# Query and key projections of the dilated attention by seven block products, with the results kept in DRAM

## The chip, the cores and the metric

The kernel runs on one core of a Trainium2 chip. The metric is the device time of one execution in microseconds (us). The engines are TensorE (PE, matmuls; PEld is its weight load), VectorE (DVE), ScalarE (ACT), GpSimd (POOL) and SyncE (SP, which here only issues DMAs). Each runs its own instructions in order.

## The reference

The kernel computes one encoder layer on 512 tokens of width 1024, in float32:

```python
x = x + 0.5 * swiglu(rmsnorm(x, g1), w1, w3, w2)      # FFN a, inner width 2816
h = rmsnorm(x, mix_norm)
pa, pq, pk, pv, pg = split(h @ w_in)                  # one input projection
# A: pa is (3 of q,k,v) x (3 groups) x (8 heads) x 64; dilations 1, 4, 16; band +-64 steps;
#    groups combined per position by a softmax over their log-sum-exps
# B: grouped-query attention, 8 query heads and 2 key heads of 128, rotary
mix = (sigmoid(pg_A) * (o_A @ P_A) + sigmoid(pg_B) * (o_B @ P_B)) @ w_out
x = x + mix
x = x + 0.5 * swiglu(rmsnorm(x, g2), ...)             # FFN b
out = rmsnorm(x, final_norm)
```

## The kernel before

**Matmuls.** Every float32 matmul is done as three in the fast format fp32r: each operand is split into a high part H and a remainder L, and `mm3` (L206 to L208) adds H·H, H·L and L·H in PSUM. Weights come in tiles of 128x1024 (512 KB): a DMA on SP's queue loads `wr`, ACT casts it to `wh` (L191), DVE computes the remainder `wl` (L192). The rings of these tiles have three buffers each, so loads, casts and remainders run ahead of PE. `order` is the list of weight tiles in the order of use.

**What sets the order.** PE's instructions are issued as the program is written; the other engines' are placed by a scheduler. Two mechanisms mix work on PE. `weave(main, fill)` takes a generator `main` of attention steps, and after each step as many units of `fill` as the step asks for. `fill` is `stream`: it goes through the list `items` of projections, one unit being three 512-column matmuls of a projection. `until(fill, item)` runs fill densely until an item is done. The gaps are GAP_S = 2 units after each pair of score tiles, GAP_V = 4 after each stage of values, GAP_B = 1 after each step of attention B, GAP_X = 8 ahead of the last values of A.

**The projections of the mixer.** `items` before: the values V of the three groups (96 units), then query and key for the four head pairs (6 chunks each, 8 units a chunk), gates 0 to 5, B's projection group 0, gates 6 and 7, B's groups 1 and 2, gates 8 to 15. A chunk of query or key is a bank of 128 features x 512 tokens; its eviction multiplies by R, the reciprocal root mean square of each token (which lies in a permuted order `Rp` for the groups with a dilation), into a tile `qk` in SBUF (L589, L591; nine buffers). Gates go to DRAM (`gate_d`) and are read back later.

**Attention A.** For each head pair `scores_a` computes S from the `qk` tiles (L648), adds the bias W and takes maxima (L653), takes exponentials on ACT (L662), exchanges maxima and sums through DRAM on SP's queue (L672 to L676; the exchange changes the layout between the groups), and computes a factor F (L678 to L688). `values_a` scales P by F (L706), transposes it on PE (T, L717) and multiplies by V (L699). The loop in `mixer` is: `until` the pair's query and key are done, scores of pair hp, values of pair hp - 1. **Attention B** is pipelined over 38 steps: scores, a transpose Tb (L829), its split PTH/PTL (L124, L125), and the matmul with v.

**Seven products.** `strassen`, `right` and `slots` are already in use for w1 and w3 in both FFNs: two feature blocks of 128 and two halves of the tokens (256 columns) and of the inner dimension (512) are the 2x2x2 blocks. The seven steps (A11, S1, S2, A12, S3, S4, A22) each take 24 matmuls of 256 columns. Some steps need sums of weight blocks: POOL's queue adds a block to a loaded one with an accumulating DMA (`wt`, L173), and DVE forms others (`ws`, L190). They also need sums of blocks of h, made once per projection (TH and TL). `slots` interleaves neighbouring pairs of columns.

## Time and profile before

| what | value |
|---|---|
| runs | 1311.12, 1311.21, 1313.84 us; median 1311.21 |
| the profiled execution | 1309.11 us, its span 1307.3 us |
| busy: PE, DVE, ACT, POOL | 1282.6, 838.1, 557.0, 111.9 us |
| granted PE clock, mean | 0.997 |
| DMA | 163.49 MB, mean 125 GB/s |

The span is the time from the first to the last instruction of the profiled execution. Busy times are sums over instructions of an engine; the forty slices and the windows show where in the span they lie. A row of instructions reads: line, engine, operation, output <- inputs, shape, count, busy time, mean of one in ns, and behind the second bar the idle time ahead of them with what ended it. A row of a timeline begins with the start and the duration.

### The profile page before, as it was taken

The numbers are of one execution on the slowest core, as the hardware profiler recorded it, in microseconds if no ns is written. First come the engines' busy times: TensorE is split into PE (matmuls) and PEld (weight loads), VectorE is DVE, ScalarE is ACT, GpSimd is POOL, SyncE is SP. The second block draws the span as 40 slices with busy tenths as digits, with TensorE's granted clock in tenths as the row PEclk, the third lists the DMA queues.
The fourth block names the chain that finished last, engine by engine and source line by source line (L and its number), as shares of the span: only waits on it lengthen the run. The fifth ranks groups of instructions, "written<-read, shape, count | busy, mean of one in ns | idle before, by whom it ended". The sixth has DMA issues, their size and how long they took to land.

```text
span 1307.3 us, 18961 instructions
## 1 busy us (share of the span) xinstructions
PE 1282.6 (98%) x7634; PEld 1112.7 (85%) x7634; DVE 838.1 (64%) x1248; ACT 557.0 (43%) x841; POOL 111.9 (9%) x100
## 2 busy tenths in 40 slices
PE   7999999999999999999999999999999999999997
PEld 5897999899789877777887778888889889988986
DVE  7884688468632346554574899655676847774775
ACT  7551355145422244244233456543475415442553
POOL 3111110010200000000022400000301000100001
PEclk9999999999999999999999999999999999999999
DMA  7865666252323223222322221245637536753321
GB/s 234 239 189 170 176 193 178 97 130 68 110 81 97 97 83 96 82 72 77 113 96 95 82 80 49 96 158 164 194 100 193 175 96 168 176 157 98 96 81 65
DMA packets 75863, 163.49 MB, mean 125 GB/s; under 512 B 11760, under 2 KB 18304, under 8 KB 75776
## 3 DMA queue, kind: packets, MB, share of 16 engines
q1 hardware_dynamic: 63984, 138.12, 32.2%
q0 software_dynamic: 11072, 23.61, 10.1%
q8 instruction: 60, 0.98, 0.3%
q10 hardware_dynamic: 720, 0.55, 0.1%
q14 instruction: 27, 0.22, 0.1%
HBM read 155.87 MB, written 10.04 MB: 127 GB/s over the span
## 4 chain that ended last, share of the span: by engine, by line
PE 85%; DVE 6%; ACT 3%; issue 3%; DMA 2%; POOL 1%; SPq 0%; POOLq 0%; DVEq 0%; ACTq 0%
PE mm L206 23%; PE mm L207 23%; PE mm L208 23%; PE Y L208 2%; PE Y L207 2%; PE Y L206 2%; ACT P L662 2%; DVE wl L192 1%; PE S L648 1%; PE X L206 1%; PE X L208 1%; PE Tb L829 1%; PE X L207 1%; PE mm L699 1%; DVE gg L405 0%
## 5 line engine op out<-in xcount | busy, mean ns | idle before, releaser
L191 ACT CAST wh<-wr 128x1024 fp32r<-128x1024 f32 x157 | 164.3, 1048 | 353.5 <-PE mm L207 243.1
L206 PE MATMUL mm<-hH,wh 128*128 128x512 f32 (+1 forms) x720 | 253.3, 352 | 4.9 <-ACT wh L953 4.9
L208 PE MATMUL mm<-hH,wl 128*128 128x512 f32 (+1 forms) x720 | 249.0, 346 | 1.4 <-DVE wl L954 0.9
L207 PE MATMUL mm<-hL,wh 128*128 128x512 f32 (+1 forms) x720 | 248.4, 345 | 1.0 <-DVE hL L328 0.9
L192 DVE TENSOR_TENSOR wl<-wr,wh 128x1024 fp32r<-128x1024 f32 x157 | 192.3, 1225 | 86.7 <-ACT wh L191 86.6
L206 PEld LDWEIGHTS mm<-hH,wh 128*128 128x128 f32 x720 | 135.7, 188 | 25.4 <-ACT wh L953 4.9
L208 PEld LDWEIGHTS mm<-hH,wl 128*128 128x128 f32 x720 | 135.5, 188 | 19.8 <-DVE wl L954 1.2
L207 PEld LDWEIGHTS mm<-hL,wh 128*128 128x128 f32 x720 | 135.6, 188 | 19.1 <-DVE hL L328 3.2
L207 PE MATMUL mm<-gg,wh 128*128 128x512 f32 (+1 forms) x376 | 143.0, 380 | 2.3 <-DVE gg L405 2.3
L206 PE MATMUL mm<-gg,wh 128*128 128x512 f32 (+1 forms) x376 | 143.4, 381 | 0.2 <-ACT gg L404 0.2
L208 PE MATMUL mm<-gg,wl 128*128 128x512 f32 (+1 forms) x376 | 142.6, 379 | 0.0
L459 DVE TENSOR_TENSOR u<-mm,R 128x512 f32<-128x512 f32 (+1 forms) x52 | 33.8, 649 | 97.2 <-PE mm L208 97.1
L206 PE MATMUL mm<-TH,wh 128*128 128x256 f32 x304 | 85.6, 281 | 2.0 <-DVE c L431 2.0
L207 PEld LDWEIGHTS mm<-gg,wh 128*128 128x128 f32 x376 | 71.0, 189 | 17.4 <-DVE gg L405 3.8
L208 PE MATMUL mm<-TH,wl 128*128 128x256 f32 x304 | 85.5, 281 | 0.0
L207 PE MATMUL mm<-TL,wh 128*128 128x256 f32 x304 | 85.4, 281 | 0.0
L206 PEld LDWEIGHTS mm<-gg,wh 128*128 128x128 f32 x376 | 70.9, 189 | 16.2 <-ACT gg L404 1.0
L208 PEld LDWEIGHTS mm<-gg,wl 128*128 128x128 f32 x376 | 70.8, 188 | 14.0
L206 PE MATMUL mm<-wh,hH 128*128 128x512 f32 x192 | 77.0, 401 | 0.0
L208 PE MATMUL mm<-wh,hL 128*128 128x512 f32 x192 | 76.2, 397 | 0.0
L207 PE MATMUL mm<-wl,hH 128*128 128x512 f32 x192 | 76.2, 397 | 0.0
L191 ACT CAST wh<-wa 128x1024 fp32r<-128x1024 f32 x38 | 39.9, 1050 | 84.4 <-PE mm L207 49.7
(198 smaller groups left out, 2652.0 us busy)
## 6 DMA issues: line engine op xcount, KB each, us to landing
wr<-in_waq SPq DMA_DIRECT2D x24, 512.0 KB, 3.5
wr<-in_w2a SPq DMA_DIRECT2D x22, 512.0 KB, 3.5
wr<-in_w2b SPq DMA_DIRECT2D x22, 512.0 KB, 3.5
wt<-in_w13b SPq DMA_DIRECT2D x20, 512.0 KB, 4.3
wa<-in_w13b SPq DMA_DIRECT2D x20, 512.0 KB, 4.3
wt<-in_w13b POOLq DMA_DIRECT2D x20, 512.0 KB, 5.9
wt<-in_w13a SPq DMA_DIRECT2D x18, 512.0 KB, 3.6
wt<-in_w13a POOLq DMA_DIRECT2D x18, 512.0 KB, 6.0
```

Source lines behind the costliest of these rows:

```text
L191: self.nc.scalar.copy(H, raw)
L192: self.nc.vector.tensor_sub(L, raw, f32(H))
L206: mm(out, lH, rH, start=start, stop=False, skip_group_check=more)
L207: mm(out, lH, rL, start=False, stop=False, skip_group_check=more)
L208: mm(out, lL, rH, start=False, stop=stop, skip_group_check=more)
L459: nc.vector.tensor_mul(u, ps, R)
L648: nc.tensor.matmul(*args, start=True, stop=True)
L662: nc.scalar.activation(sl, sl, AF.Exp, bias=SO[:, 0, li, h:h + 1], scale=1.0, accum_out=SO[:, 0, li, 2 + h:3 + h])
L699: nc.tensor.matmul(oc, v, p, start=st, stop=sp)
L829: nc.tensor.transpose(pt[:, 128 * j:128 * j + 128], P[h, j][:, 128 * k:128 * k + 128], self.ident)
```

## The change

The mixer now begins with `project_qk`. It runs the three value projections of `stream`, and between their units twelve small steps (`tq_steps`) in which ACT and DVE form TQ, four sums of blocks of x times the norm's gain (H and L parts). Then 20 of the 24 query and key chunks are computed by `strassen`: ten (head pair, group) pairs of PAIRS, whose query and key chunk form the two feature blocks, in the order of PAIRS. `evict` collects the products (ACT copies, DVE additions), scales by R (permuted in `acc`, which takes the place of `Rp`) into tiles `qo` of one buffer, and stores each to DRAM (`qk_d`) on POOL's queue. `fetch(hp)` reads a head pair's tiles back into `qk`, on POOL's queue too. The last four chunks (head pair 3, groups 1 and 2) stay in `items` as they were. Now `items` behind the values is: gates 0 to 2, the remaining query and key chunks, gates 3 to 8, B's groups 0, 1 and 2, gates 9 to 15. `until` ahead of the scores is left only for head pair 3, GAP_X goes from 8 to 4, and V gets a pool of its own that is freed ahead of attention B.

```diff
@@ -19,8 +19,10 @@
 BUFS = {"wr": 3, "wa": 3, "ws": 2, "wt": 3, "wh": 3, "whx": 1}
 EARLY = 4
 GROUPS = {"a": (4, 8, 16, 22), "b": (2, 8, 16, 22)}
+PAIRS = ((0, 0), (1, 0), (0, 1), (0, 2), (1, 1), (1, 2), (2, 0), (3, 0), (2, 1), (2, 2), (3, 1), (3, 2))
+NSQ = 10
 STEPS = ("A11", "S1", "S2", "A12", "S3", "S4", "A22")
-GAP_X = 8
+GAP_X = 4
 GAP_V = 4
 GAP_S = 2
 GAP_B = 1
@@ -81,16 +83,21 @@
         self.acc = c.tile([128, T], F32, name="acc")
         self.open_h()
         self.gate_d = self.dram.tile([16, 128, T], F32, name="gate_d")
-        self.items = ([("v", g) for g in range(3)] + [("qk", h) for h in range(4)] + [("g", j) for j in range(6)]
-                      + [("b", 0), ("g", 6), ("g", 7), ("b", 1), ("b", 2)] + [("g", j) for j in range(8, 16)])
-        span = {"v": ("wav", 4), "qk": ("waq", 6), "g": ("wg", 1), "b": ("wb", 4)}
+        self.qk_d = self.dram.tile([2 * NSQ, 128, T], F32, name="qk_d")
+        self.items = ([("v", g) for g in range(3)] + [("sw", 0)] + [("g", j) for j in range(3)]
+                      + [("qk", f) for f in range(NSQ, 12)] + [("g", j) for j in range(3, 9)]
+                      + [("b", g) for g in range(3)] + [("g", j) for j in range(9, 16)])
+        span = {"v": ("wav", 4), "qk": ("waq", 2), "g": ("wg", 1), "b": ("wb", 4)}
         self.order = self.ffn_order("a")
         for kind, n in self.items:
+            if kind == "sw":
+                self.order += [("swq", at) for at in self.slots(range(0, NSQ, 2))]
+                continue
             name, m = span[kind]
             self.order += [(name, m * n + i) for i in range(m)]
         self.order += [("wab", i) for i in range(12)] + [("wo", i) for i in range(8)]
         self.order += self.ffn_order("b")
-        self.raws, self.tiles, self.used, self.wx = {}, [], 0, None
+        self.raws, self.tiles, self.used, self.wx, self.TQ = {}, [], 0, None, None
         self.rings = {k: [] for k in BUFS}
         self.index = {it[:2]: n for n, it in enumerate(self.order)}
         self.kind = [self.home(it) for it in self.order]
@@ -267,8 +274,11 @@
     def right(self, step, k):
         lo, hi = slice(0, 256), slice(256, 512)
         d, cs = {"A11": (k, lo), "A12": (4 + k, lo), "S3": (k, hi), "S4": (4 + k, hi)}.get(step, (0, 0))
-        if cs:
+        if cs and not (self.TQ and step == "S3"):
             return self.hH[d][:, cs], self.hL[d][:, cs]
+        if self.TQ:
+            c = {"S1": 0, "S3": 1, "A22": 2, "S2": 3}[step]
+            return tuple(t[:, k, c, :] for t in self.TQ)
         c = {"S1": 0, "A22": 1, "S2": 2}[step]
         return self.TH[:, c, k, :], self.TL[:, c, k, :]
 
@@ -363,10 +373,10 @@
...
-        nc.vector.tensor_copy(self.Rp.rearrange("p (r m) -> p r m", r=4), self.R.rearrange("p (m r) -> p r m", r=4))
+        nc.vector.tensor_copy(self.acc.rearrange("p (r m) -> p r m", r=4), self.R.rearrange("p (m r) -> p r m", r=4))
         pr = self.aux("rps")
         for r in range(4):
-            nc.tensor.transpose(pr[:, r:r + 1], self.Rp[0:1, 128 * r:128 * r + 128], self.ident[0:1, 0:1])
+            nc.tensor.transpose(pr[:, r:r + 1], self.acc[0:1, 128 * r:128 * r + 128], self.ident[0:1, 0:1])
         nc.vector.tensor_copy(self.r[:, 4:8], pr[:, 0:4])
...
@@ -580,21 +590,16 @@
 
                 yield from self.token("wav", 4 * n, toks, done)
             elif kind == "qk":
-                qk = {}
-                for j, (part, g) in enumerate([(0, 0), (1, 0), (0, 1), (1, 1), (0, 2), (1, 2)]):
-
-                    def done(ps, part=part, g=g):
-                        t = self.ap.tile([128, T], F32, tag="qk", name="qk", bufs=9)
-                        if g == 0:
-                            nc.vector.tensor_mul(t, ps, self.R)
-                        else:
-                            nc.vector.tensor_mul(t.rearrange("p (r m) -> p r m", r=4),
-                                                 ps.rearrange("p (m r) -> p r m", r=4),
-                                                 self.Rp.rearrange("p (r m) -> p r m", r=4))
-                        qk[part, g] = t
-
-                    yield from self.feat("waq", 6 * n + j, done)
-                self.qk[n] = qk
+                hp, g = PAIRS[n]
+                for part in range(2):
+
+                    def done(ps, hp=hp, part=part, g=g):
+                        t = self.qk[hp][part, g] = self.ap.tile([128, T], F32, tag="qk", name="qk", bufs=9)
+                        nc.vector.tensor_mul(t.rearrange("p (r m) -> p r m", r=4),
+                                             ps.rearrange("p (m r) -> p r m", r=4),
+                                             self.acc.rearrange("p (r m) -> p r m", r=4))
+
+                    yield from self.feat("waq", 2 * n + part, done)
             elif kind == "g":
 
                 def done(ps, j=n):
@@ -607,6 +612,107 @@
                 toks = [(lambda t, i=i: t[:, 128 * i:128 * i + 128]) for i in range(4)]
                 yield from self.token("wb", 4 * n, toks, lambda i, b, grp=n: self.rope(grp, i, b))
             self.past.add((kind, n))
+
+    def fetch(self, hp):
+        for f, (h, g) in enumerate(PAIRS[:NSQ]):
+            if h == hp:
+                for part in range(2):
+                    t = self.qk[hp][part, g] = self.ap.tile([128, T], F32, tag="qk", name="qk", bufs=9)
+                    self.nc.gpsimd.dma_start(t, self.qk_d[2 * f + part])
+
+    def tq_steps(self, cp):
+        nc = self.nc
+        raw = {}
+
+        def put(k):
+            raw[k] = cp.tile([128, 4, 256], F32, tag="c1", name="Traw")
+            for e in range(2):
+                d = k + 4 * e
+                nc.scalar.activation(raw[k][:, 2 * e:2 * e + 2], self.x[d].rearrange("p (a n) -> p a n", a=2), AF.Copy,
+                                     scale=self.par[:, G_MIX + d:G_MIX + d + 1])
+
+        def sums(k):
+            b = [raw[k][:, c] for c in range(4)]
+            neg = lambda o, x, y: nc.vector.scalar_tensor_tensor(o, x, -1.0, y, op0=ALU.mult, op1=ALU.subtract)
+            nc.vector.tensor_sub(b[0], b[0], b[1])
+            nc.vector.tensor_sub(b[1], b[3], b[1])
+            neg(b[3], b[3], b[0])
+            neg(b[2], b[3], b[2])
+
+        def part(k):
+            H, L = (t[:, k] for t in self.TQ)
+            nc.scalar.copy(H, raw[k])
+            nc.vector.tensor_sub(L, raw[k], f32(H))
+
+        return [lambda fn=fn, k=k: fn(k) for k in range(4) for fn in (put, sums, part)]
+
+    def project_qk(self):
+        nc, tc = self.nc, self.tc
+        with ExitStack() as ctx:
+            pool = lambda n, **k: ctx.enter_context(tc.tile_pool(name=n, reuse_waits="tile", **k))
+            tp = pool("qT", bufs=1)
+            self.TQ = [tp.tile([128, 4, 4, 256], F32R, name=f"TQ{c}") for c in "HL"]
+            self.wx = pool("wxq", bufs=1)
+            cp, qp = pool("cq", bufs=2), pool("qo", bufs=1)
+            steps = self.tq_steps(cp)
+            hooks = {7: self.stat_r, 12: self.stat_R, 17: self.stat_p}
+            for n, _ in enumerate(self.stream(self.items[:3])):
+                if n in hooks:
+                    hooks[n]()
+                if n > 20 and n % 4 == 0 and steps:
+                    steps.pop(0)()
+            assert not steps
+            c = {}
+
+            def scaled(dst, src, a, perm, neg):
+                src, dst = src.rearrange("p (j n) -> p j n", j=2), dst.rearrange("p (j n) -> p j n", j=2)
+                R = (self.acc if perm else self.R).unsqueeze(1).to_broadcast([128, 2, T])
+                if perm:
+                    src = src.rearrange("p j (m r) -> p j r m", r=4)
+                    dst, R = (t.rearrange("p j (r m) -> p j r m", r=4)[:, :, :, 64 * a:64 * a + 64] for t in (dst, R))
+                else:
+                    dst, R = (t[:, :, 256 * a:256 * a + 256] for t in (dst, R))
+                if neg:
+                    for j in range(2) if perm else (slice(0, 2),):
+                        nc.vector.scalar_tensor_tensor(dst[:, j], src[:, j], -1.0, R[:, j], op0=ALU.mult, op1=ALU.mult)
+                else:
+                    nc.vector.tensor_mul(dst, src, R)
+
+            def store(f, part, t):
+                i = 2 * f + part
+                nc.gpsimd.dma_start(self.qk_d[i:i + 3:2].rearrange("c p n -> p c n"), t.rearrange("p (c n) -> p c n", c=2))
+
+            def evict(f, step, ps):
+                perm = PAIRS[f][1] > 0
+                if step == "A11":
+                    c[f] = (cp.tile([128, 1024], F32, tag="c1", name="c1"), self.tmp.tile([128, T], F32, tag="t", name="c2"))
+                c1, c2 = c[f][:2]
+                lo, hi = c1[:, :T], c1[:, T:]
+                if step == "A11":
+                    nc.scalar.copy(lo, ps)
+                elif step == "S1":
+                    nc.scalar.copy(c2, ps)
+                elif step == "S2":
+                    nc.scalar.copy(hi, ps)
+                elif step == "A12":
+                    nc.vector.tensor_add(lo, ps, lo)
+                elif step == "S3":
+                    nc.vector.tensor_add(c2, ps, c2)
+                elif step == "S4":
+                    nc.vector.tensor_add(hi, ps, hi)
+                    o = qp.tile([128, 1024], F32, tag="qo", name="qo")
+                    scaled(o, lo, 0, perm, False)
+                    scaled(o, hi, 1, perm, False)
+                    store(f, 0, o)
+                else:
+                    o = qp.tile([128, 1024], F32, tag="qo", name="qo")
+                    scaled(o, ps, 0, perm, True)
+                    scaled(o, c2, 1, perm, True)
+                    store(f, 1, o)
+
+            for _ in self.strassen("q", range(0, NSQ, 2), evict):
+                pass
+            self.wx = self.TQ = None
 
     def until(self, fill, item):
         while item not in self.past:
@@ -853,31 +959,33 @@
 
     def mixer(self):
         nc, tc = self.nc, self.tc
-        self.past, self.qk = set(), {}
-        fill = self.stream()
+        self.past, self.qk = set(), {h: {} for h in range(4)}
+        vctx = ExitStack()
+        vp = vctx.enter_context(tc.tile_pool(name="V", bufs=1, side="right", reuse_waits="tile"))
+        self.V = [vp.tile([128, 4, 512], F32, name=f"V{g}") for g in range(3)]
+        self.project_qk()
+        fill = self.stream(self.items[4:])
         with tc.tile_pool(name="oA", bufs=1, reuse_waits="tile") as oa:
             self.oH = [oa.tile([128, T], F32R, name=f"oH{h}") for h in range(4)]
             self.oL = [oa.tile([128, T], F32R, name=f"oL{h}") for h in range(4)]
             with tc.tile_pool(name="A", bufs=1, reuse_waits="tile") as ap:
                 self.ap = ap
-                self.Rp = ap.tile([128, T], F32, name="Rp")
-                self.V = [ap.tile([128, 4, 512], F32, name=f"V{g}") for g in range(3)]
-                for n, fn in ((7, self.stat_r), (5, self.stat_R), (5, self.stat_p)):
-                    for _ in range(n):
-                        next(fill)
-                    fn()
                 held = None
+                self.fetch(0)
                 for hp in range(4):
-                    self.until(fill, ("qk", hp))
+                    if hp == 3:
+                        self.until(fill, ("qk", 11))
                     res = []
                     self.weave(self.scores_a(hp, res), fill)
+                    if hp < 3:
+                        self.fetch(hp + 1)
                     if held:
                         self.weave(self.values_a(hp - 1, *held), fill)
                     held = res
                 for _ in range(GAP_X):
                     next(fill)
                 self.weave(self.values_a(3, *held), fill)
-            self.until(fill, ("g", 5))
+            vctx.close()
             with tc.tile_pool(name="B", bufs=1, reuse_waits="tile") as bp:
                 self.qH = bp.tile([128, 8, T], F32R, name="qH")
                 self.qL = bp.tile([128, 8, T], F32R, name="qL")
@@ -1034,7 +1142,8 @@
         out["w2" + s] = np.concatenate([block_chunks(w2[128 * lo:128 * hi]) for lo, hi in zip(ends, ends[1:])])
     w = p["w_in"][0]
     wa = w[:, :4608].reshape(D, 3, 3, 512)
-    qk = wa[:, 0:2].reshape(D, 2, 3, 4, 128).transpose(0, 3, 2, 1, 4).reshape(D, 24 * 128)
+    qk = wa[:, 0:2].reshape(D, 2, 3, 4, 128)
+    qk = np.concatenate([qk[:, part, g, h] for h, g in PAIRS for part in range(2)], axis=1)
     out["waq"] = feat_chunks(qk)
     out["wav"] = token_chunks(wa[:, 2].reshape(D, 1536))
     wq = w[:, 4608:5632].reshape(D, 8, 128)[:, :, half].reshape(D, 1024)
```

More of the change, by code (lines that the diff above doesn't have):

```diff
@@ L161, in load @@
             return True
-        w = self.a["w13" + name[2]]
+        w = self.a["waq" if name[2] == "q" else "w13" + name[2]]
         dst = raw.rearrange("p (a c) -> p a c", a=2)
@@ L566, in bias_spread, with stream @@
             self.nc.gpsimd.dma_start(self.zd[h], bass.AP(tensor=src.tensor, offset=src.offset, ap=[[0, 128], [1, NV]]))
-    def stream(self):
+    def stream(self, items):
         nc = self.nc
-        for kind, n in self.items:
+        for kind, n in items:
             if kind == "v":
```

## The prediction

> **What bounds the kernel now.** I read the page first: the span, the busy times, the slices of PE and the chain that ended last.
>
> ```profile
> span 1307.3 us, 18961 instructions
> PE 1282.6 (98%) x7634; PEld 1112.7 (85%) x7634; DVE 838.1 (64%) x1248; ACT 557.0 (43%) x841; POOL 111.9 (9%) x100
> PE   7999999999999999999999999999999999999997
> PE 85%; DVE 6%; ACT 3%; issue 3%; DMA 2%; POOL 1%; SPq 0%; POOLq 0%; DVEq 0%; ACTq 0%
> ```
>
> TensorE sets the time: it is busy in 98% of the span, every slice but the first and last is at 9, and 85% of the chain is its own. A matmul less is worth its time, and each microsecond in which the new order leaves PE without work is lost, because only 24.7 us of the span are idle now. Then I read windows by stage (columns: window, busy time and instructions of PE, PEld, DVE, ACT, POOL, granted clock, DMA share, GB/s): the query and key projection as it is now, and the two FFNs, which already use seven block products with 256-column matmuls.
>
> ```profile
> 430.00:463.00 33.00, 33.00 (x143) 26.74 (x142) 11.30 (x12) 6.04 (x6) 0.00 (x0) 1.00 0.29 96
> 164.00:204.00 40.00, 40.00 (x343) 40.00 (x343) 31.56 (x32) 21.41 (x24) 4.75 (x4) 1.00 0.73 185
> 1095.00:1130.00 35.00, 35.00 (x312) 35.00 (x311) 28.12 (x29) 19.40 (x22) 2.41 (x2) 1.00 0.73 189
> ```
>
> PE without a gap gives 33.00/143 = 0.231 us for a 512-column matmul, 40.00/343 = 0.117 and 35.00/312 = 0.112 for a 256-column one (a window counts matmuls that only reach into it, so each is right to 1%).
>
> **The matmuls.** 20 of the 24 query and key chunks change. Before, each is 24 matmuls of 512 columns: 480 x 0.231 = 110.8 us. After, five column pairs of seven steps with 24 matmuls of 256 columns: 840, at 0.117 98.3 us, at 0.112 94.1 us. I take 0.1155, nearer the slower row, 97.0 us: **-13.8 us** (-12.5 to -16.7). Everything else that PE computes is unchanged, so the rest of the sum is PE time without work.
>
> **The end of the projection** (+4.1 us). On POOL's queue stand the stores of results to DRAM (qk_d<-qo), the weight sums (wt<-in_waq), and the fetches that bring one head pair's tiles back (qk<-qk_d). After the change:
>
> ```order
> L683 DMA qk_d<-qo 128x2x512 x2
> L180 DMA wt<-in_waq 128x2x512 x2
> L683 DMA qk_d<-qo 128x2x512 x5
> L621 DMA qk<-qk_d 128x512 x5
> L683 DMA qk_d<-qo 128x2x512
> L621 DMA qk<-qk_d 128x512 x15
> ```
>
> The first fetch is put behind all stores but one, and the tile pool of the attention reuses the memory of TQ, the block sums, so that it also waits for the last step's matmuls. On PE the first scores come right behind those:
>
> ```order
> L213 MATMUL mm<-TQH,wh 128x256
> L214 MATMUL mm<-TQL,wh 128x256
> L215 MATMUL mm<-TQH,wl 128x256
> L754 MATMUL S<-qk 128x256 x4
> L213 MATMUL mm<-hH_96,wh 128x512
> L214 MATMUL mm<-hL_104,wh 128x512
> ```
>
> PE runs in order, so the gate projection behind S (hH, wh) can't fill the wait. S needs two fetches, query and key. The nearest rows:
>
> ```profile
> 117.12 4.18 POOL L566 DMA_DIRECT2D zd<-vd  x8 [1.62 <-issue]
> gate_d<-z SPq DMA_DIRECT2D x16, 256.0 KB, 2.0
> zg<-gate_d SPq DMA_DIRECT2D x16, 256.0 KB, 2.9
> wt<-in_w13b POOLq DMA_DIRECT2D x20, 512.0 KB, 5.9
> zd<-vd POOLq DMA_DIRECT2D x8, 446.5 KB, 11.5
> ```
>
> One issue on POOL takes 4.18/8 = 0.52 us; 256 KB land in 2.0 us (to DRAM) and 2.9 (from it), POOL's 512 KB sums in 5.9. Two issues and 2.0: 3.0 us; and 2.9: 3.9; and 5.9: 6.9. I take 3.9 and 0.2 for the store's issue ahead: 4.1 (3.0 to 6.9). Before, the tiles were ready in SBUF: no such wait.
>
> **The softmax of the first head pair** (+8.0 us). The transposes of head pair 0's probabilities (T) wait for exponentials, for an exchange of sums through DRAM, and for a scaling. The chain in the trace before, head pair 0, then the end of head pair 3's (columns: start, us, engine, line, operation):
>
> ```profile
> 471.86 1.16 PE L648 MATMUL S<-qk 64*128 64x128 f32 x16
> 472.95 0.50 PE L206 MATMUL mm<-hH,wh 128*128 128x512 f32 x1
> 474.79 1.28 ACT L662 ACT_TABLE_LOAD   x1
> 476.38 0.51 ACT L662 ACTIVATE P<-P,SO 128x256 f32<-128x256 f32 x1 [0.31 <-DVE SO L658]
> 483.97 0.19 ACT L662 ACTIVATION_READ_ACCUMULATOR P<-P,SO 128x1 f32 x1
> 487.65 1.13 SPq L676 DMA_DIRECT2D SO<-d  x2
> 492.48 0.17 DVE L678 TENSOR_TENSOR MN<-SO 128x16 f32<-128x16 f32 x1
> 494.17 1.60 DVE L706 TENSOR_SCALAR P<-P,F 128x256 f32<-128x256 f32 x6
> 502.00 1.14 PE L648 MATMUL S<-qk 64*128 64x256 f32 x8
> 512.52 1.03 PE L717 MATMUL T<-ident,P 128*128 128x128 f32 x8
> 603.95 1.16 PE L648 MATMUL S<-qk 64*128 64x128 f32 x16
> 605.04 0.50 PE L206 MATMUL mm<-hH,wh 128*128 128x512 f32 x1
> 624.38 1.14 DVE L706 TENSOR_SCALAR P<-P,F 128x256 f32<-128x256 f32 x4
> 631.95 1.04 PE L717 MATMUL T<-ident,P 128*128 128x128 f32 x8
> ```
>
> From the end of the last scores (472.95, where PE's next matmul starts) to the first scaling 21.2 us pass in head pair 0, from 605.04 to 624.38 19.3 us in head pair 3, and two scalings of 0.3 each come before T. Now what PE has to do meanwhile. Before:
>
> ```order
> L648 MATMUL S<-qk 128x128 x8
> L206 MATMUL mm<-hH_103,wh 128x512
> L207 MATMUL mm<-hL_111,wh 128x512
> L208 MATMUL mm<-hH_103,wl 128x512
> L206 MATMUL mm<-hH_96,wh 128x512
> L207 MATMUL mm<-hL_104,wh 128x512
> L208 MATMUL mm<-hH_96,wl 128x512
> ```
>
> 126 such projection matmuls follow (29.05 us, 472.95 to 502.00), then the next pair's scores. After:
>
> ```order
> L754 MATMUL S<-qk 128x128 x8
> L213 MATMUL mm<-hH_102,wh 128x512
> L214 MATMUL mm<-hL_110,wh 128x512
> L215 MATMUL mm<-hH_102,wl 128x512
> L213 MATMUL mm<-hH_103,wh 128x512
> L214 MATMUL mm<-hL_111,wh 128x512
> L215 MATMUL mm<-hH_103,wl 128x512
> L754 MATMUL S<-qk 128x256 x4
> ```
>
> Six matmuls (1.39 us) and then the next pair's scores at once. Those with their fill take 512.52 - 502.00 = 10.5 us, as before: cover 11.9. With head pair 3's chain PE stands 19.3 + 0.6 - 11.9 = 8.0 us; with head pair 0's 9.9; 1.5 less than the first, 6.5, where the maxima need not queue behind a weight's remainder on DVE. I take 8.0 (6.5 to 9.9). Later pairs have some 20 us of values in between, and the last one's first T, at 631.95 in the trace, comes 2.8 us earlier by the shorter gap (4 units of 0.69 us for 8): 629.2, still behind 625.0, so nothing.
>
> **The clock** (+2.5 us). The trace has one gap of PE in a dense stage, within the first window here (4.00 - 2.13 = 1.87 us):
>
> ```profile
> 1151.00:1155.00 4.00, 2.13 (x19) 1.96 (x18) 4.00 (x5) 1.08 (x2) 0.00 (x0) 1.00 1.01 245
> 1155.00:1158.40 3.40, 3.40 (x17) 3.40 (x16) 2.83 (x4) 2.25 (x3) 0.00 (x0) 0.50 0.81 317
> 1158.40:1162.00 3.60, 3.60 (x17) 2.89 (x17) 3.56 (x4) 1.85 (x2) 0.00 (x0) 1.00 0.57 164
> ```
>
> After it PE runs 3.4 us at half the clock: 1.7 us lost. Two new gaps, both longer, would cost 3.4 together; at no cost 0. I take 2.5. The Trainium skill ("TensorE: Matmul & The Clock Gate", Part 1, the HAM clock gate) says that the clock halves after at least one idle window of about 3.4 us that runs freely, and asks for no idle over some 3 us; this speaks against the change. By that rule only the 8 us gap is sure to pay, 1.7 us; the row, where 1.87 us sufficed, goes further than the rule.
>
> **The end of attention B** (+1.2 us). Projection matmuls also fill attention B. The new list has 31 units of three left there for 38 steps, so the last seven steps are bare:
>
> ```order
> L935 MATMUL Tb<-ident,Pb 128x128 x4
> L213 MATMUL mm<-PTH,vH 128x512
> L214 MATMUL mm<-PTL,vH 128x512
> L215 MATMUL mm<-PTH,vL 128x512
> L935 MATMUL Tb<-ident,Pb 128x128 x4
> ```
>
> Before, three projection matmuls stand behind each. Tb goes through ACT (PTH) and DVE (PTL) before its matmul:
>
> ```profile
> 835.49 0.60 PE L829 MATMUL Tb<-ident,Pb 128*128 128x128 f32 x4
> 836.12 0.59 ACT L124 CAST PTH<-Tb 128x512 fp32r<-128x512 f32 x1 [1.25 <-PE Tb L829]
> 836.74 0.69 DVE L125 TENSOR_TENSOR PTL<-Tb,PTH 128x512 fp32r<-128x512 f32 x1 [1.14 <-ACT PTH L124]
> ```
>
> PTL is done 1.94 us after Tb starts. A bare step is 1.15 us of PE and the matmul that wants PTL stands 1.8 us behind its Tb: some 0.1 per step, and 0.6 at the last, which has only itself to hide: 1.2 (0.5 to 2.5).
>
> **Inside the projection** (+1.0 us). DVE's work for a column pair:
>
> ```profile
> L192 DVE TENSOR_TENSOR wl<-wr,wh 128x1024 fp32r<-128x1024 f32 x157 | 192.3, 1225 | 86.7 <-ACT wh L191 86.6
> L190 DVE TENSOR_TENSOR ws<-ws,wa 128x1024 f32<-128x1024 f32 x19 | 24.4, 1282 | 0.6
> L429 DVE TENSOR_TENSOR c<-X,c 128x512 f32<-128x512 f32 x19 | 13.0, 686 | 3.8 <-PE X L208 3.8
> L591 DVE TENSOR_TENSOR qk<-mm,Rp 128x512 f32<-128x512 f32 x16 | 11.1, 692 | 38.7 <-PE mm L208 38.7
> ```
>
> Seven remainders, two sums, three additions and four scalings are 8.6 + 2.6 + 2.1 + 2.8 = 16.1 us, against 168 x 0.1155 = 19.4 of PE. The results have one buffer, qo, so the scaling of A22 waits for the store of S4's. About 2.4 us of remainders lie between; a store that lands L us after its issue holds DVE for L - 2.4, and PE pays from 16.1 + L - 2.4 = 19.4 on, L = 5.7. The 5.9 row stands just at it: 0.2 for each of five pairs, 1.0. No wait at all gives 0; the 11.5 row gives 5.8 a pair.
>
> **Sum.** -13.8 + 4.1 + 8.0 + 2.5 + 1.2 + 1.0 = +3.0 us. The profiled execution took 1309.1 us (1.8 outside the span) and would take 1312.1; it is 2.1 below the median of the runs, 1311.2, and on that footing the forecast is **1314.2 us**.
>
> **Rivals.** *The gain survives* (faster). The softmax starts 1.5 us earlier, the fetches land in 2.0, the clock stays up, the store hides: -13.8 + 3.0 + 6.5 + 0.6 = -3.7, 1307.5. For it: the chain of head pair 3 holds waits behind other DVE work. Against: the halved clock in the trace. *Nothing to see.* Matmuls at the 0.112 row and no clock loss, with the stalls as forecast: -16.7 + 4.1 + 8.0 + 1.2 + 1.0 = -2.4, 1308.8; or clock loss at 1.7 besides, 1310.5. For it: that row has the same block products. Against: the other FFN's has them too. *The stores bind* (slower). At L = 8.7, between 5.9 and 11.5, each pair pays 3.0, 15 in all instead of 1: 1328. For it: one buffer, and POOL issues weight sums in the same queue. Against: the 11.5 row had eight broadcasts at once. *The change does not do what it says*: 256-column matmuls at more than half the time of the 512s. 0.117 against 0.231 leaves it little.
>
> **How the numbers follow.** What a measurement here can tell from no change is about 0.2%, 2.6 us, so no change is 1308.6 to 1313.8. The forecast has 0.46 (its own range 1311 to 1320, two thirds of it slower by over 2.6 us), the surviving gain 0.18, nothing to see 0.22, the stores 0.12, the last 0.02. Slower: 0.32 of the forecast's, 0.05 of the second rival's (its terms may be off by their own bounds), 0.12 of the stores' and 0.01, together 0.50. Same: 0.14, 0.15 and 0.01, together 0.30. Faster: the first rival's 0.18 and 0.02 of the second's, 0.20. The range goes from the surviving gain to a part of the stores' case: 1306 to 1323.
>
> **What would show it.** PE's matmuls in the projection at 0.1155 each; a PE gap of about 4 us ahead of the first S, ended by a DMA of qk; a gap of about 8 ahead of the first T, ended by DVE's P; granted clock 0.5 behind one or both; small gaps at PTL in the last seven steps. Wrong would be: no gap ahead of T (another order of fill than the one read), DVE waiting on qo for more than 4 us in a pair, or matmuls of 256 columns well off 0.115.

## The result: slower by 1.3%, against a forecast of 0.2%

The changed kernel takes 1328.24 us (median; 1327.08 to 1329.53), the kernel before 1311.16 beside it. The ratio is 1.0129, with a 95% interval of 1.0108 to 1.0150. The direction was forecast, the size was not: +3.0 us was predicted, +17.1 measured, and 1328.2 lies above the range of 1306 to 1323.

The profiled execution of the changed kernel has a span of 1326.0 us, 18.7 more than before. The page, line by line against the one shown of before:

```profile
span 1326.0 us, 19937 instructions
PE 1281.0 (97%) x7994; PEld 1127.0 (85%) x7994; DVE 886.6 (67%) x1314; ACT 588.1 (44%) x883; POOL 142.8 (11%) x140
PE   8999999999999999788999999999999999999997
PEclk9999999999999999888999999999999999999998
PE 79%; DVE 7%; issue 5%; DMA 4%; ACT 3%; POOL 1%; SPq 0%; POOLq 0%; DVEq 0%; ACTq 0%
```

PE is busy for about as long as before (1281.0 us, 1282.6 before), though it has some 11 us less to compute. The slices 17 to 19 show why: PE is idle there and its granted clock is down, and a matmul at half clock counts as busy for twice as long. In the chain PE falls from 85% to 79%, while DMA, issue and DVE take its place.

The windows of the changed kernel from the projection to the second head pair's values (columns as before: window, busy time and instructions of PE, PEld, DVE, ACT, POOL, granted clock, DMA share, GB/s):

```profile
429.71:531.17 101.46, 100.01 (x840) 99.45 (x839) 72.92 (x80) 44.00 (x50) 14.54 (x15) 1.00 0.64 174
531.17:538.98 7.81, 0.28 (x3) 0.11 (x2) 2.81 (x5) 0.00 (x0) 4.81 (x9) 0.83 0.93 313
538.98:545.00 6.02, 6.02 (x28) 3.96 (x29) 1.90 (x9) 0.00 (x0) 1.52 (x4) 0.66 1.02 369
557.00:565.36 8.36, 6.80 (x43) 5.14 (x43) 4.50 (x27) 4.49 (x20) 1.06 (x2) 0.80 0.44 155
565.36:572.00 6.64, 0.40 (x2) 0.03 (x1) 4.12 (x15) 6.08 (x23) 0.00 (x0) 0.88 0.88 251
572.00:578.50 6.50, 6.50 (x24) 5.51 (x25) 4.26 (x16) 3.32 (x14) 0.00 (x0) 0.60 0.20 34
608.50:613.11 4.61, 0.22 (x2) 0.00 (x0) 0.12 (x1) 4.61 (x20) 0.00 (x0) 0.81 0.21 60
613.11:619.00 5.89, 5.89 (x25) 4.75 (x26) 0.44 (x3) 0.32 (x1) 0.00 (x0) 0.57 0.08 4
```

The projection takes 101.46 us in place of 110.8, of which PE works 100.0: 840 matmuls at 0.119. Then come three windows in which PE does nearly nothing (the second, fifth and seventh), and each is followed by one at a lower clock. The waits view of the changed kernel, rows out of four windows (engine and instruction, what it waited for, us in total, times, longest), names who ended each wait:

```profile
PE S L754 <- DMA qk<-qk_d: 7.5, 1, 7.5
DVE P L759 <- DMA W<-zd: 2.9, 1, 2.9
PE S L754 <- DVE MX L759: 1.6, 1, 1.6
PE T L823 <- DVE P L812: 6.2, 1, 6.2
PE mm L805 <- ACT PT L825: 4.4, 1, 4.4
```

These are, in order: the first scores for their fetch (7.7 us from PE's last matmul slot to the first score); the third pair of scores of head pair 1, whose banks wait for VectorE, which waits for the bias W of that head pair (1.8); the first transposes for the scaled P (6.4); and, in the values of head pair 1, matmuls that wait for a PT copied by ScalarE (4.6). The last one stood in no term of the prediction. ScalarE's timeline, and PE's beside it:

```profile
604.83 0.51 ACT L768 ACTIVATE P<-P,SO 128x256 f32<-128x256 f32 x1
...
612.00 0.49 ACT L768 ACTIVATE P<-P,SO 128x256 f32<-128x256 f32 x1
612.40 0.19 ACT L768 ACTIVATION_READ_ACCUMULATOR P<-P,SO 128x1 f32 x1
612.50 0.94 ACT L825 COPY PT<-T 128x512 f32<-128x512 f32 x2
```

```profile
603.91 1.03 PE L823 MATMUL T<-ident,P 128*128 128x128 f32 x8
607.54 0.82 PE L823 MATMUL T<-ident,P 128*128 128x128 f32 x6
608.28 0.43 PE L805 MATMUL mm<-PT,V 128*64 128x128 f32 x2
613.11 1.97 PE L805 MATMUL mm<-PT,V 128*64 128x128 f32 x14 [4.39 <-ACT PT L825]
```

The transposes of head pair 1 come 1.5 us behind the last scores of head pair 2. The sixteen exponentials of head pair 2 stand ahead of the copies in ScalarE's order and keep it until 612.50.

Put together for the stretch from the start of the mixer to the first matmul behind attention B (479.9 us before, 500.6 after, +20.7):

| term | predicted | measured |
|---|---|---|
| matmuls of the projection, 110.8 less | -13.8 | -10.8 (100.0 busy) |
| PE's waits inside the projection | +1.0 | +1.5 |
| ahead of the first scores | +4.1 | +7.7 |
| ahead of the first transposes | +8.0 | +8.2 (1.8 for W, 6.4 for P) |
| behind the exponentials | none | +4.6, less 1.3 for shorter waits of this kind before |
| half clock behind these gaps | +2.5 | +8.9 (6.02 x 0.34 + 8.36 x 0.20 + 6.50 x 0.40 + 5.89 x 0.43) |
| end of attention B | +1.2 | +2.1 |
| sum | +3.0 | +20.9 |

The rest of the kernel, whose code is the same, was 2.1 us shorter in this execution (465.7 us for 467.8): the gap of 1.87 us in the last FFN that the prediction showed is 0.8 us in it, and the granted clock does not fall behind it.

### The profile page after: what moved, and what is told of

Its sections match the earlier page's. It is cut to its first block, busy times and chain, and to the rows that moved or that the text cites. A ratio compares the mean times of both kernels' runs of the same rounds, so it can differ in the third digit from the quotient of the medians.

```text
span 1326.0 us, 19937 instructions
## 1 busy us (share of the span) xinstructions
PE 1281.0 (97%) x7994; PEld 1127.0 (85%) x7994; DVE 886.6 (67%) x1314; ACT 588.1 (44%) x883; POOL 142.8 (11%) x140
## 4 chain that ended last, share of the span: by engine, by line
PE 79%; DVE 7%; issue 5%; DMA 4%; ACT 3%; POOL 1%; SPq 0%; POOLq 0%; DVEq 0%; ACTq 0%
PE mm L213 21%; PE mm L214 20%; PE mm L215 20%; PE Y L213 3%; PE Y L214 3%; PE Y L215 3%; DVE wl L199 1%; PE S L754 1%; PE X L213 1%; PE X L214 1%; PE X L215 1%; PE mm L805 1%; ACT P L768 1%; PE Tb L935 1%; DMA wr<-in_w2b 1%
## 5 line engine op out<-in xcount | busy, mean ns | idle before, releaser
L199 DVE TENSOR_TENSOR wl<-wr,wh 128x1024 fp32r<-128x1024 f32 x142 | 173.4, 1221 | 61.6 <-ACT wh L198 61.0
L213 PE MATMUL mm<-hH,wh 128*128 128x256 f32 (+1 forms) x600 | 204.1, 340 | 4.8 <-ACT wh L1061 4.8
L215 PE MATMUL mm<-hH,wl 128*128 128x256 f32 (+1 forms) x600 | 199.2, 332 | 1.0 <-DVE wl L199 0.5
L214 PE MATMUL mm<-hL,wh 128*128 128x256 f32 (+1 forms) x600 | 199.2, 332 | 0.7 <-DVE hL L338 0.7
L213 PEld LDWEIGHTS mm<-hH,wh 128*128 128x128 f32 x600 | 114.6, 191 | 20.0 <-ACT wh L1061 4.8
L215 PEld LDWEIGHTS mm<-hH,wl 128*128 128x128 f32 x600 | 114.5, 191 | 13.5 <-DVE wl L199 0.9
L214 PEld LDWEIGHTS mm<-hL,wh 128*128 128x128 f32 x600 | 114.5, 191 | 11.9 <-DVE hL L338 2.3
L214 PEld LDWEIGHTS mm<-gg,wh 128*128 128x128 f32 x376 | 70.8, 188 | 18.7 <-DVE gg L415 5.1
L215 PEld LDWEIGHTS mm<-gg,wl 128*128 128x128 f32 x376 | 70.8, 188 | 13.9
L199 DVE TENSOR_TENSOR wl<-wt,wh 128x1024 fp32r<-128x1024 f32 x48 | 58.6, 1221 | 34.5 <-ACT wh L198 34.3
L198 ACT CAST wh<-ws 128x1024 fp32r<-128x1024 f32 x48 | 50.4, 1051 | 69.8 <-PE mm L214 52.2
L198 ACT CAST wh<-wt 128x1024 fp32r<-128x1024 f32 x48 | 50.3, 1050 | 69.9 <-PE mm L214 39.9
```

Source lines behind the costliest of these rows:

```text
L198: self.nc.scalar.copy(H, raw)
L199: self.nc.vector.tensor_sub(L, raw, f32(H))
L213: mm(out, lH, rH, start=start, stop=False, skip_group_check=more)
L214: mm(out, lH, rL, start=False, stop=False, skip_group_check=more)
L215: mm(out, lL, rH, start=False, stop=stop, skip_group_check=more)
```

## The experiments

The theory after this reading: seven products pay, but the projection that used to run densely around the scores was also cover, for four chains (the fetch, W, the softmax, the copies behind exponentials), and each uncovered chain costs its gap and then some 2 us of half clock. The main rival of this theory: the projection itself loses, by its matmul rate, its stores and its sums.

### Cover put back (e1_fill)

V of the third group moves from ahead of the seven products to behind them (32 units of three matmuls): 11 ahead of the first scores, 8 within them, the rest ahead of the second. The twelve steps of TQ start earlier to find their place among fewer units.

```diff
-        self.items = ([("v", g) for g in range(3)] + [("sw", 0)] + ...
+        self.items = ([("v", g) for g in range(2)] + [("sw", 0), ("v", 2)] + ...
...
-                if n > 20 and n % 4 == 0 and steps:
+                if n > 14 and n % 4 == 0 and steps:
...
                 self.fetch(0)
+                for _ in range(11):
+                    next(fill)
                 for hp in range(4):
+                    if hp == 1:
+                        self.until(fill, ("v", 2))
```

> The changed kernel, but the third value projection (32 units of three matmuls) is no longer done ahead of the seven products: 11 of its units run between them and the first scores, 8 within the first scores, 13 between the first and the second scores. Theory (the loss is PE without work ahead of the first scores, 7.8 us, ahead of W and T of the second head pair, 1.8 and 6.4, and in the bare end of attention B, 2.1, with the half clock behind the first three, some 5.5): all of this goes, 1328.2 - 23.6 = about 1305 us, and the gap of 4.6 us ahead of a PT in the values stays. Rival (the loss lies in the projection itself, its matmul rate and its stores): at most the 7.8 and its clock go, 1318 or more.

Measured: 1304.94 us, ratio to before 0.9952 (0.9936 to 0.9968), so the change turns from 1.3% slower to 0.5% faster by the order alone. The window over the first two head pairs' scores and first transposes, and before it the projection:

```profile
410.59:513.00 102.41, 100.34 (x841) 99.54 (x840) 74.09 (x80) 43.99 (x50) 15.00 (x16) 1.00 0.65 175
513.00:560.00 47.00, 46.90 (x276) 39.64 (x275) 27.37 (x106) 19.72 (x57) 11.80 (x22) 1.00 0.72 237
```

PE is busy in 46.90 of 47.00 us where three gaps were, at full clock. The projection still takes 102.4: the rival that the loss lies there falls. The bare end of attention B stayed, against the expectation; the eight units that were won ran densely ahead of attention B, and were not kept for it. Against the expectation too, the gap ahead of a PT fell from 4.6 us to 1.4, and the granted clock behind it was 1.00. The two misses pull in opposite ways, so the total of about 1305 us is met partly by luck.

### Copies of PT by VectorE (e2_pt)

```diff
-                cp = nc.scalar.copy if h else nc.vector.tensor_copy
+                cp = nc.scalar.copy if h and hp == 3 else nc.vector.tensor_copy
```

> The changed kernel, but for head pairs 0 to 2 both copies of a transposed block (PT) are made by VectorE, where the second was made by ScalarE. Theory (the 4.6 us gap is a copy that stands behind 16 exponentials of the next head pair in ScalarE's order): the gap goes, with the 3.4 us at half clock behind it (1.7): 1328.2 - 6.3 = about 1322 us. Rival (PE would wait there anyway, for the scaling of P or for the exchange of sums): within 1 us of 1328.

Measured: 1322.53 us, 5.7 below the changed kernel, near the 6.3 expected. The matmuls behind the transposes at the same place, in this kernel:

```profile
608.55 0.82 PE L823 MATMUL T<-ident,P 128*128 128x128 f32 x6
609.29 1.09 PE L805 MATMUL mm<-PT,V 128*64 128x128 f32 x16
```

All sixteen run at once. So the wait was for ScalarE's order and not for data.

### Both (e3_both)

> Both edits together. Theory: the gains add, about 1299 us, some 12 us faster than the kernel before, which is the matmuls' 11.2 us and the gap in the last FFN. Rival (time is only moved to another wait): above 1305.

Measured: 1304.59 us, ratio 0.9936 (0.9910 to 0.9961). The expectation of 1299 failed, and the time lies just under the rival's bound of 1305. The gains do not add in the medians: e1_fill already has a smaller gap at that place (1.4 us for 4.6; what made it smaller was not taken apart). The profiled execution is at 1303.3 us. The projection takes 103.82 us here, 2.4 more than in the changed kernel (row below, at the experiment with two buffers).

### Useless matmuls in the gaps (e4_spin)

```diff
+    def spin(self, n):
+        ps = self.bank()
+        for _ in range(n):
+            self.nc.tensor.matmul(ps, self.hH[0][:, 0:128], self.hH[1], start=True, stop=True)
...
                 self.fetch(0)
+                self.spin(30)
```

and `spin(6)`, `spin(25)`, `spin(17)` at the other three gaps.

> The changed kernel with useless matmuls of 512 columns put into its gaps: 30 ahead of the first scores (6.9 us), 6 ahead of the third pair of scores of head pair 1 (1.4), 25 ahead of the first transposes (5.8), 17 ahead of the matmuls that wait for a PT (3.9); each less than the gap that it stands in. No wait is shortened. Theory (behind each gap PE runs at half clock for some 3.4 us, about 7.5 us lost in all): the clock stays up and the kernel becomes faster by 6 to 7.5 us in spite of the added work, about 1321 us. Rival (a slow start behind a gap is a property of the first matmuls, not of a clock that idling turned down): no gain, 1328 or a little more.

Measured: 1323.79 us, 4.4 faster than the changed kernel with 78 matmuls more; that is less than the 6 to 7.5 expected of the whole kernel. The gaps themselves show more: from the first score to the first matmul behind attention B 313.35 us pass (539.63 to 852.98) in place of 321.35 (538.98 to 860.33), 8.0 less. The rest of the kernel, which the edit does not touch, was 4.1 us longer in this profile than in that of the changed kernel. The windows at the same places:

```profile
532.00:539.63 7.63, 6.99 (x33) 5.48 (x31) 2.23 (x5) 0.00 (x0) 3.93 (x8) 1.00 0.95 319
539.63:545.00 5.37, 5.37 (x34) 3.45 (x36) 2.75 (x16) 0.00 (x0) 3.06 (x6) 1.00 1.04 377
569.01:573.00 3.99, 3.99 (x24) 3.33 (x24) 3.99 (x16) 3.99 (x18) 0.00 (x0) 1.00 0.39 122
613.00:617.00 4.00, 4.00 (x33) 3.38 (x33) 3.53 (x12) 0.84 (x3) 0.00 (x0) 1.00 0.32 93
```

The first scores wait as long as before (539.63 here, 538.98 there), but the granted clock is 1.00 in all these windows, and also behind the second gap (558.05 to 563.00). The half clock is shown to be the idling's doing.

### What made the fetch late (e5_split, e9_store_moved)

The chain of waits of the changed kernel ahead of the first scores (start, us, what), and from the view of the fetches' line their times from issue to landing:

```profile
532.09 0.58 POOL qk L621
532.67 6.17 DMA qk<-qk_d
538.98 2.04 PE S L754 x7
```

```profile
DMA to landing us min/median/max: 2.9/5.8/7.4
```

The shortest, 2.9, is the last fetch of all, issued alone at 597.47; the two that the first scores need take 5.6 and 6.2. First suspicion: the three fetches issued right behind them.

```diff
-                self.fetch(0)
+                self.fetch(0, (0,))
...
+                        if hp == n == 0:
+                            self.fetch(0, (1, 2))
```

with one column of a tile first written by VectorE out of the first scores, so that the fetch has to come later.

> The changed kernel, but ahead of the first scores only the two tiles that these need (query and key of group 0) are fetched; the other four tiles of head pair 0 are fetched when the first pair of scores has been taken over (a column of one of them is first written by VectorE, so that the fetch has to wait). Theory (the first fetch lands late, 5.8 us in place of the 2.9 that I took, because five fetches, a store and W loads share the DMA engines, 0.93 busy at 313 GB/s in the 7.8 us): the two land in 3 to 4 us and PE waits 5 to 6 us ahead of the first scores in place of 7.7. Rival (a fetch on this queue takes 5.8 us by itself): 7.5 us or more. The time of the whole run is not the test, since the third pair of scores may wait in turn for the fetches that were put off.

Measured, in one execution (1331.59 us): the gap is 7.8 us, and the two tiles still land 5.8 and 6.3 us after their issue. The suspicion falls. The profiled chain:

```profile
531.04 0.58 POOL qk L623
531.62 6.26 DMA qk<-qk_d
538.01 2.04 PE S L757 x7
```

The Trainium skill ("DMA: Bandwidth & Descriptors", Queues, rings and completion order) says that a DMA engine takes turns between its queues packet by packet, and that on each engine descriptors are consumed in ring order. The run agrees with this: what stands behind in the same queue did not hold up what stands ahead (5.8 and 6.3 us without it, 5.6 and 6.2 with it). So the next suspicion was what was issued just ahead, POOL's store of 512 KB (0.7 us ahead) and SP's weight tile of 512 KB (in the same microsecond).

```diff
+                    if f == 0:
+                        store(NSQ - 2, 0, o)
+                    if f < NSQ - 2:
-                    store(f, 0, o)
+                        store(f, 0, o)
```

> The changed kernel, but the store of the last column pair's first half, which is issued 0.7 us ahead of the first fetch, is left out; in its place another tile is stored to the same rows at the first column pair, so that as many bytes move in all (queries of head pair 2, groups 1 and 2, are wrong by it). Theory (a fetch lands late because of the 512 KB store and the 512 KB weight tile that were issued just ahead of it; fetches issued behind it don't matter, by e5_split): the first two fetches land in 3 to 4.5 us in place of 5.6 to 6.2, and PE waits 4.5 to 6 us ahead of the first scores in place of 7.7. Rival (the weight tile and W alone do it): 7 us or more.

Measured, in one execution (1335.28 us): the first tile lands after 4.0 us, the second after 5.6, and PE waits 6.7 us in place of 7.7.

```profile
537.46 0.51 POOL qk L621
538.01 5.59 DMA qk<-qk_d
543.74 1.61 PE S L757 x5
```

The store is worth 1 us of the wait, less than the theory wanted and more than the rival's: 0.6 by the earlier landing of the second tile, the rest because POOL issues the fetch sooner. The edit moved something else as well: VectorE waits 0.8 us for `qo` there in place of 3.3, so the next store is issued 1.9 us behind the first fetch and not 5.5. What makes up the rest, against the 2.9 of a fetch alone, is not shown; a weight tile and the W tiles of this head pair were moving beside it. It was not taken apart further, since cover hides most of it: in the last kernel below PE waits 1.4 us for it.

### Two buffers for the results (e6_qo2)

The only buffer `qo` makes VectorE wait for its store. In the changed kernel's projection:

```profile
DVE qo L677 <- DMA qk_d<-qo: 10.0, 4, 3.8
DVE qo L679 <- DMA qk_d<-qo: 4.7, 4, 1.3
```

There was no room for a second one; keeping V of the third group in the attention's own pool (possible once it is computed behind the projection) makes it.

```diff
-            cp, qp = pool("cq", bufs=2), pool("qo", bufs=1)
+            cp, qp = pool("cq", bufs=2), pool("qo", bufs=2)
...
-        self.V = [vp.tile([128, 4, 512], F32, name=f"V{g}") for g in range(3)]
+        self.V = [vp.tile([128, 4, 512], F32, name=f"V{g}") for g in range(2)]
...
+                self.V.append(ap.tile([128, 4, 512], F32, name="V2"))
```

> The kernel of e3_both with two buffers for the scaled results (qo) in place of one; the room comes from the values of group 2, which are kept in the attention's own pool. Theory (the gaps inside the projection, some 4 us in e3_both, come from VectorE waiting up to 4.8 us for a store out of the only buffer): gaps under 1 us, no wait of VectorE for a store above 1 us, 1304.6 - 3 = about 1301 us. Rival (the accumulating DMAs of the weight sums are late by themselves): the gaps stay, within 1 us of e3_both.

Measured: 1299.27 us, ratio 0.9904 (0.9881 to 0.9928). The projection in e3_both, and in this kernel:

```profile
408.19:512.01 103.82, 100.43 (x842) 99.64 (x840) 74.14 (x80) 44.00 (x50) 15.09 (x16) 1.00 0.64 173
```

```profile
406.58:506.41 99.83, 99.66 (x841) 99.46 (x840) 75.48 (x82) 44.00 (x50) 14.96 (x16) 1.00 0.65 180
```

4.0 us shorter, with PE busy in 99.66 of 99.83, and no wait of VectorE for a store is left in it. The stores behind one buffer were a real cost, some 1.5 to 4 us over the five column pairs. The rival falls: the sums go by the same accumulating DMAs here and hold nothing up, so they were not late by themselves. How VectorE's wait became PE's was not taken apart.

### One gate kept for attention B (e7_best)

```diff
-                      + [("qk", f) for f in range(NSQ, 12)] + [("g", j) for j in range(3, 9)]
-                      + [("b", g) for g in range(3)] + [("g", j) for j in range(9, 16)])
+                      + [("qk", f) for f in range(NSQ, 12)] + [("g", j) for j in range(3, 8)]
+                      + [("b", g) for g in range(3)] + [("g", j) for j in range(8, 16)])
```

> The kernel of e6_qo2 with gate 8 moved behind the projections of attention B, so that eight more units of fill are left for attention B. Theory: no gap ahead of the last PTL matmuls but the last one (0.4), 1 to 2 us faster than e6_qo2, about 1300 us. Rival (the gaps at the end come from the split itself): no difference.

Measured: 1296.88 us, ratio to before 0.9891 (0.9867 to 0.9915). This is faster than both kernels of this case: 14.0 us below the kernel before, some 31 below the changed one, and 2.4 below e6_qo2, where 1 to 2 were expected. All waits of PE from shortly before the end of the projection to the end of attention B (the waits view of this kernel, PE alone):

```profile
PE Tq L908 <- DVE xk L894: 2.0, 2, 1.0
PE S L754 <- DMA qk<-qk_d: 1.4, 1, 1.4
PE Tb L935 <- DVE Pb L929: 0.7, 1, 0.7
PE mm L213 <- DVE oL L848: 0.5, 1, 0.5
```

No PTL is left. The changed kernel had these two in PE's timeline at the end of attention B:

```profile
857.20 0.50 PE L214 MATMUL mm<-PTL,vH 128*128 128x512 f32 x1 [0.19 <-DVE PTL L132]
859.76 0.50 PE L214 MATMUL mm<-PTL,vH 128*128 128x512 f32 x1 [0.23 <-DVE PTL L132]
```

### The copies in the kernel before (e8_before_pt)

> The kernel before with the same PT edit as e2_pt (VectorE makes both copies for head pairs 0 to 2). Theory (there 126 or more projection matmuls run between the exponentials of a head pair and the values of the one ahead of it, so the copies never stand behind exponentials): no change, within 0.2% of before. Rival (the edit is a gain of its own, apart from the change): 3 us or more faster.

Measured: 1308.09 us, ratio 0.9980 (0.9969 to 0.9991): 2.8 us faster, on the bound between the two. A gain clear of no change is shown, so the theory's reason fails. In the trace of before the copy does stand behind exponentials of the next head pair, in the values of each of the first three head pairs:

```profile
521.64 0.49 ACT L662 ACTIVATE P<-P,SO 128x256 f32<-128x256 f32 x1
522.14 0.45 ACT L719 COPY PT<-T 128x384 f32<-128x384 f32 x1
522.64 0.88 PE L699 MATMUL mm<-PT,V 128*64 128x128 f32 x14 [0.46 <-ACT PT L719]
```

So also there PE stood for copies by ScalarE, 1.4 us over three times, and the edit takes that away. The dense projection had kept this wait short; it had not kept it away.

What are the seven products worth? Outside the mixer the code is the same in all these kernels, yet their profiled executions differ there by some us (465.7 to 469.4 us behind attention B), and the kernel before has medians of 1311.2, 1312.9 and 1310.9 us in the three sets of runs. So the table also has, from one profile each, the stretch from the mixer's first matmul to the first matmul behind attention B:

| kernel | median, us | stretch, us |
|---|---|---|
| before | 1311.2 | 479.9 |
| before, copies by VectorE (e8_before_pt) | 1308.1 | 477.3 |
| changed | 1328.2 | 500.6 |
| e1_fill | 1304.9 | 476.2 |
| e2_pt | 1322.5 | 493.7 |
| e3_both | 1304.6 | 474.3 |
| e4_spin | 1323.8 | 491.8 |
| e6_qo2 | 1299.3 | 471.5 |
| e7_best | 1296.9 | 469.1 |

The fair base for the seven products is e8_before_pt. Against it e7_best gains 11.2 us by the medians, but only 8.2 by the stretch; of the 11.0 us between the two profiled spans, 2.8 lie in stages whose code is the same. The projection itself takes 99.4 us in the trace of e7_best for 110.8, 11.4 less. So some 3 us of its saving are lost again within the mixer, 1.9 of them in waits that e8_before_pt does not have, for the fetch and for `oL`; the agreement of 11.2 with 11.4 is partly chance.

## Why the prediction was wrong, step by step

The sum came out 17.9 us too low: 6.4 in the clock, 3.6 ahead of the first scores, 3.3 in the copies behind exponentials, for which it had no term, 3.0 in the matmuls, and 1.6 in the rest. Of these, 7.5 go back to one step: the gaps for W and for the copies were not foreseen, and to the 3.3 come 4.2 of half clock behind the two (8.36 x 0.20 + 5.89 x 0.43).

**The matmuls** (-13.8, measured -10.8; -11.4 without stores in the way). What failed here is the choice of 0.1155 between 0.117 and 0.112: 0.1183 to 0.119 was measured, above both. Why this stage is 1% slower than the first FFN's is open.

**The end of the projection** (+4.1, measured 7.7, beyond its bound of 6.9). The place, the order of POOL's queue and the two issues were right. The landing was mis-sized: 2.9 us is that of a fetch alone, and the two that counted took 5.6 and 6.2 with a store and a weight tile moving. The DMA share of 0.93 in that window could have been foreseen from the order of issues: store, weight tile, W and five fetches are issued within 3 us.

**The softmax of the first head pair** (+8.0, measured 8.2). Right in size, partly by luck: from the last scores of head pair 0 (549.90) to the first scaling (571.50) 21.6 us passed, as in that head pair's own row of before (21.2) and not 19.3, while PE's work in between took 13.9 us and not 11.9, part of it at half clock. It came as two gaps: 1.8 us for W, a chain that the prediction had not named (two buffers of W, loaded again behind the last scores of the head pair ahead, landing 6 us later), and 6.4 for P.

**"Later pairs have some 20 us of values in between"**, costed at nothing: the step that failed outright. It followed only the chain to the scaled P, where it holds. It did not ask what else the dense projection kept nearly apart on ScalarE: the exponentials of one head pair and the PT copies of the other (0.5 us of waiting each time before). 4.6 us of gap, and 2.5 of half clock; e2_pt took back 5.7 by the medians and 6.9 in the stretch of the table.

**The clock** (+2.5, measured 8.9). Two gaps were priced at no more than 1.7 each. There were four, and each cost 1.7 to 2.6 us: PE worked at half clock for 3.3 to 5.2 us behind them (twice the loss in each window), where the one row of before gave 3.4. Even the gap of 1.8 us paid, like the 1.87 us in the trace of before; by the rule of the Trainium skill ("TensorE: Matmul & The Clock Gate", Part 1, the HAM clock gate: a whole idle window of about 3.4 us) it need not have, so the row was the better guide.

**The end of attention B** (+1.2, measured 2.1) and **inside the projection** (+1.0, measured 1.5) were right in kind. That VectorE would wait on `qo` was right too: 14.7 us in all, most of it without harm. The size inside the projection is luck: the sum has stores that land after 5.9 us, and they landed after 3.9 in the median, for which it would have nothing to pay. One of the prediction's signs of being wrong, more than 4 us of waiting on `qo` in a pair, came true as well: 3.8 and 1.3 us in the second pair.

**The rivals.** The case of the stores (1328) has the measured time, by accident: the stores cost 1.5 to 4 us, and not 15. No case had a chain that the removed cover had hidden besides those of the sum. The range was built from the bounds of the terms, and two of them were too narrow (fetch, clock) and one was missing.

## What to carry to other kernels

Work that is moved out of the middle of an in-order queue was also the cover of everything around it: ahead of such a move, list for every engine which two of its jobs it kept apart, not only which chain it hid. In a kernel like this one, price a gap on PE as its length and some 2 us of half clock behind it, from under 2 us of idling on (1.8 and 1.9 us paid, 1.4 did not); where nothing useful is at hand, even useless matmuls in the gaps were worth 4.4 us here, 8 in the stretch that they stood in. A saving of 11 us in the projection was real and was first turned into a loss of 17; keeping 22 us of independent projection behind the new stage, and splitting a queue or a buffer that two chains shared, gave most of it back.

## What the runs showed of the hardware

A 256 KB fetch from DRAM on POOL's queue landed in 2.9 us when alone and in 5.6 to 6.2 with 512 KB ahead of it in the queue and 512 KB on another; leaving three later fetches away changed nothing (5.8 and 6.3), and without the 512 KB ahead in its own queue it was 4.0 and 5.6. PE's granted clock fell to half behind gaps of 7.7, 6.4, 4.6 and 1.8 us, and stayed at 1.00 when the same gaps were filled with matmuls whose result nobody reads; behind single waits of 1.4 us (e1_fill, e7_best) it stayed at 1.00 too.
